# The last pair of experts as unsplit float32, through four 32-column groups of TensorE

## Chip, cores, metric

One Trainium2 chip, one of its eight cores. The metric is the device time of one execution in microseconds, median over runs. Before the change it is 2039.08 us (three runs, 2037.84 to 2042.18).

## What is computed

Two layers over 256 latent tokens and 256 context tokens of 1024 channels. Each layer mixes tokens (attention, chunked gating, Fourier), then applies a feed-forward part: dense in layer 0, a mixture of experts in layer 1. Only the mixture is touched here; it is the last thing in the program. Cut from the reference:

```python
def _swiglu(x, wg, wu, wd):
    return (jax.nn.silu(x @ wg) * (x @ wu)) @ wd

def _moe_swiglu(x, router, wg, wu, wd):
    logits = (x @ router).astype(jnp.float32)
    top_v, top_i = lax.top_k(logits, TOP_K)          # 2 of 8 experts
    top_w = jax.nn.softmax(top_v, axis=-1)
    ...
    for e in range(N_EXPERTS):
        out = out + gates[..., e:e + 1] * _swiglu(x, wg[e], wu[e], wd[e])
```

An expert has 3 x 1024 x 3584 float32 weights, 44 MB. With the given inputs the reference's router sends 200, 100, 95, 68, 42, 6, 1 and 0 tokens to the eight experts, in order of size.

## The kernel before

**Items and pairs.** Tokens are gathered by expert into items of at most 128, biggest experts first, and items are taken in pairs `a` to `d`. Here `a` is both items of the 200-token expert, `b` the 100 and 95, `c` the 68 and 42, `d` the 6 and the 1. `route` computes a number `kind` on the chip that picks one of three schedules; the first holds where pair `a` is of one expert and items 5, 6 and 7 have 64 tokens at most.

**Weights.** They come in half units of 512 KiB (128 partitions x 1024 float32): 56 per expert for gate and up (two k-tiles of 512 columns each), 28 for down (one k-tile of 1024 columns). For pairs `b`, `c`, `d` both items' half units of a step go into one 1 MiB buffer `rp`, by two transfers issued on SP's queue (line 1334); for pair `a` two successive half units of its one expert share a buffer (line 1326). There are five such buffers, so SP waits, in order, until the buffer used five steps earlier is free.

**Split.** TensorE multiplies in float32r. To keep float32 accuracy each half unit is split into hi (ScalarE, line 1311) and lo = raw - hi (VectorE, line 1312), five buffers of each; the lo of a half unit is the last reader of its raw. The generator `expert_halves` yields these parts in the order of the schedule, two ahead of their use.

**Products.** A full item takes three products per k-tile, hi*hi, hi*lo and lo*hi (`mm3`, lines 241 to 243; for pair `a`, which runs transposed with the weights stationary, line 1355). An item of at most 64 tokens puts the hi and lo parts of its tokens side by side as one 128-column stationary operand, which leaves two products (lines 1405, 1406) and a later addition of the two 64-row halves (lines 1399, 1400). Pair `c` has one full and one such item ('mixed'); pair `d` has two ('small', `gate_up_small`).

**Order.** A schedule is a string: `du01+au3` means gate/up chunks 0 and 1 of pair `d` interleaved evenly with chunk 3 of pair `a`; `d` as second letter is the down projection, `p` the gathering of a pair's tokens. Inside each schedule's block a scheduler then orders the instructions of each engine. `weighed` scales the down projection's result by the tokens' gate weights into hi and lo, `scatter` multiplies it by one-hot rows back to token places (line 1260), `residual_half` adds it to x (lines 809, 810), and `g_final` follows the last pair with the norm (lines 1284, 1287) and the output.

Of the kernel before, what the change touches and what calls it, by code (L numbers as in the profile page):

```python
# [9 lines left out]
F32 = mybir.dt.float32  # L10
# [18 lines left out]
    'bu0123456 cp ap bd0123456 cu01+au0 cu23+au1 cu4 cu56+ad01 dp cd0123456+au2 du01+au3 ad2 du2+au4 '  # L29
    'du3+au5 du4+au6 du56+ad3456 dd0123456',  # L30
# [10 lines left out]
class Act:  # L41
    """A [256 tokens, 128*n channels] activation, channel-major, as hi and lo parts, 4 k-tiles to a tile."""
# [10 lines left out]
class Joint:  # L53
    """Channel-major hidden activations of both streams, blocks 0, 1 of L, then of C, 2 k-tiles to a tile."""
# [10 lines left out]
class Pair:  # L65
    """Two items. kind:
    'whole': the hidden activations are kept until all of them are there, and then go through the down projection,
    'one': both are of one expert, and the hidden activations go through the down projection in parts,
    'small': both have 64 tokens at most, whose hi and lo parts are the two halves of the stationary operand, so that
    the hi and lo parts of the weights take two passes, and the sums of both halves are taken afterwards,  # L70
    'mixed': the first as in 'whole', the second as in 'small'."""

    def __init__(self, kind):
        self.kind, self.flat, self.aT, self.sums, self.work, self.done = kind, {}, {}, None, {}, 0
        self.shared = None
        self.small = {'small': (True, True), 'mixed': (False, True)}.get(kind, (False, False))
# [15 lines left out]
class Side:  # L92
    """Work that is emitted a step at a time between the weight units of the main stream."""
# [45 lines left out]
class Net:  # L139
# [135 lines left out]
    def linear(self, act, units, n, outs, k0=0, first=True, last=True):  # L275
        """out[b] += act[:, k0 * 128:]^T @ units; outs: (block, psum)"""
# [19 lines left out]
    def stats_by_sum(self, x, sums):  # L296
        """minus the mean [128, 1] and 1 / std [128, 1] over the 1024 channels of x; sums: of the channels, one or two"""
# [11 lines left out]
    def stats(self, x, st=None):  # L309
        """mean [128, 1] and 1 / std [128, 1] over the 1024 channels of x; st: the statistics of its halves"""  # L310
# [16 lines left out]
    def row(self, src, r=None):  # L327
        """a [1024] DRAM row on all partitions"""
# [27 lines left out]
    def mod_bias(self):  # L356
        """the biases of the modulation by channel, one added where they are of a scale"""
# [96 lines left out]
    def mod_col(self, l, s, which, kt):  # L454
        """(scale + 1, shift) of channel tile kt: which=0 before the mixer, 1 before the FFN"""
# [14 lines left out]
    def x_turned(self, xn, kt2):  # L470
        """PSUM [128, 2, 256]: channel tiles 2 kt2 and 2 kt2 + 1 of the normalised tokens"""
# [15 lines left out]
    def g_modulate(self, act, tiles, l, s, which, t4=None, kind=None):  # L487
        """act gets the modulated tiles that tiles(kt2) gives, [128, 2, 256] each"""
        for kt2 in range(4):
            if kt2 % 2 == 0:  # L490
                if kind == 'small':
                    act.h.append(self.t4([128, 4, 256], F32R))
                else:
                    self.act_tiles(act, t4)
# [3 lines left out]
            if kind == 'small':  # L498
                self.split_halves(act.h[-1][:, o, :], t)
            elif kind == 'mixed':  # L500
# [15 lines left out]
    def modulate(self, works, l, s, which, queue=None):  # L516
        """norm and modulation of stream s once the works are done, as side work"""
# [13 lines left out]
    def headnorm(self, z, nh, out, w, blk):  # L531
        """out [128, nh, 64] = rms-normed heads of z, gained, rotated when blk is a latent block"""
# [84 lines left out]
    def g_attention(self, s, sq, skv):  # L617
# [103 lines left out]
    def g_transposed(self, act, src, n, scale=1.0, c0=0):  # L721
        """append channel tiles c0..c0+n of a token-major activation to act: src(block, channel tile) is [128, 128]"""
# [58 lines left out]
    def out_kept(self, aT, ps, w, b, u):  # L781
        """block b times unit u of an output projection whose halves w are on chip"""
# [5 lines left out]
    def merge(self, l, y, n, hh, ts, acc, first, mid=None):  # L788
        """acc += 2 sigmoid(z) * (y @ w_branch), ts = tanh(z / 2); mid: what to emit after the products"""
# [31 lines left out]
    def finish(self, s, psums, rows, alpha=ALPHA, queue=None):  # L821
        """the residual now, the norm as side work"""
# [13 lines left out]
    def mixer(self, l, s, act, kv_c=None, early=None):  # L836
        """kv_c: keys and values of the context; early: what to emit while the first half of act is worked on"""
# [73 lines left out]
    def ffn(self, sL, sC):  # L911
        """the dense SwiGLU of both streams, on each weight unit together where that is possible: the first columns
        are worked on for L alone, when C may not be there yet, and the last rows of the down projection for L and
        then for C, so that L can go on. Returns what does the last rows of a stream."""
# [3 lines left out]
        def up(c, ss):  # L918
            """512 columns, the last time 256, as channels by tokens"""
# [89 lines left out]
    def moe_consts(self):  # L1009
# [7 lines left out]
        it = ld('iota', [128, 4, 128])  # L1017
# [927 lines left out]
```

## Time and profile before

| | us |
|---|---|
| median of three runs | 2039.08 |
| span of the profiled execution, first to last instruction | 2036.6 |
| TensorE busy in it | 1965.7 |
| VectorE busy | 1537.9 |
| ScalarE busy | 1258.9 |

The profiled execution's own time is its span, 2036.6 us; what lies around the span is not in the profile, and the median of the timed runs is 2.5 us above it. Busy TensorE time is that of overlapping records, so a share near 100% says that there is always a matmul in the array, not that the array is at its peak. The mixture of experts takes the part from about 1110 us to the end; the transfers of all its weights are 308 MB.

### The profile page before, as it was taken

Reading aid. Unit: us, or ns where it says so; the run is one execution under the profiler, and the core shown is the slowest. Engines: PE = TensorE matmul, PEld = TensorE weight load, DVE = VectorE, ACT = ScalarE, POOL = GpSimd, SP = SyncE. Lnnn points to the kernel's source line nnn. Section 1 sums busy time; section 2 is a strip of 40 time slices with the busy share of each in tenths; the row PEclk is TensorE's granted clock in tenths of the full one; section 3 lists DMA queues with packets and bytes.
Section 4 is the critical chain, followed back from the end, with each engine's and each line's share of the span. In section 5 each row is a group of like instructions: output and inputs, shape, how many; then the busy total and the mean of one; then the engine's idle time right before and its main releaser. Section 6 shows DMA issues by size and latency. Waiting matters only on the chain. (4 is left out here: it accounts for less than half of the span.)

```text
span 2036.6 us, 30525 instructions
## 1 busy us (share of the span) xinstructions
PE 1965.7 (97%) x10833; PEld 1627.3 (80%) x10833; DVE 1537.9 (76%) x2148; ACT 1258.9 (62%) x1653; POOL 56.6 (3%) x54
## 2 busy tenths in 40 slices
PE   6999999999999999999996999999999999999995
PEld 3788877788979979878885777888877888898863
DVE  3877776778243343798787888899898889999897
ACT  4667545655222222466763877887777878777775
POOL 0100010000000000111000000000000000000000
PEclk9999999999999999999997999999999999999998
DMA  9653566677443343444441999898899898999995
GB/s 337 242 192 138 191 243 231 220 272 261 187 175 145 145 145 128 175 158 166 145 167 61 402 358 349 325 370 318 333 349 351 324 382 325 340 326 340 336 352 203
DMA packets 119353, 519.91 MB, mean 255 GB/s; under 512 B 14688, under 2 KB 15584, under 8 KB 96144
## 3 DMA queue, kind: packets, MB, share of 16 engines
q1 hardware_dynamic: 119184, 517.80, 69.2%
q8 instruction: 89, 1.46, 0.3%
q14 instruction: 80, 0.66, 0.1%
HBM read 516.63 MB, written 1.11 MB: 254 GB/s over the span
## 5 line engine op out<-in xcount | busy, mean ns | idle before, releaser
L1312 DVE TENSOR_TENSOR lo<-rp,hi 128x1024 fp32r<-128x1024 f32 x588 | 688.3, 1219 | 66.2 <-ACT hi L1311 61.4
L1311 ACT ACTIVATE hi<-rp 128x1024 fp32r<-128x1024 f32 (+1 forms) x588 | 595.2, 1055 | 123.4 <-PE mm L1355 46.1
L242 PE MATMUL mm<-lo,t 128*128 128x512 f32 (+1 forms) x1560 | 608.4, 390 | 3.0 <-DVE lo L1312 2.0
L243 PE MATMUL mm<-hi,t 128*128 128x512 f32 (+1 forms) x1560 | 605.7, 389 | 0.7 <-DVE t L236 0.7
L241 PE MATMUL mm<-hi,t 128*128 128x512 f32 (+1 forms) x1560 | 587.8, 395 | 7.6 <-ACT hi L235 3.6
L236 DVE TENSOR_TENSOR lo<-raw,hi 128x1024 fp32r<-128x1024 f32 x268 | 325.8, 1219 | 266.3 <-ACT hi L235 265.5
L235 ACT ACTIVATE hi<-raw 128x1024 fp32r<-128x1024 f32 x268 | 282.6, 1058 | 373.6 <-PE mm L243 192.1
L241 PEld LDWEIGHTS mm<-hi,t 128*128 128x128 f32 x1560 | 292.3, 188 | 88.1 <-issue 17.5
L242 PEld LDWEIGHTS mm<-lo,t 128*128 128x128 f32 x1560 | 293.6, 188 | 67.4 <-DVE lo L1312 8.2
L243 PEld LDWEIGHTS mm<-hi,t 128*128 128x128 f32 x1560 | 293.6, 188 | 61.7 <-DVE t L236 1.3
L942 PE MATMUL mm<-t,hi 128*128 128x256 f32 x1408 | 236.6, 285 | 0.0
L942 PEld LDWEIGHTS mm<-t,hi 128*128 128x128 f32 x1408 | 200.9, 191 | 14.4 <-issue 8.4
L1406 PE MATMUL mm<-lo,t 128*128 128x512 f32 x504 | 191.7, 407 | 5.7 <-DVE lo L1312 5.7
L1405 PE MATMUL mm<-hi,t 128*128 128x512 f32 x504 | 188.5, 399 | 0.7 <-ACT hi L1311 0.7
L1355 PE MATMUL mm<-t,hi 128*128 128x256 f32 x896 | 158.4, 280 | 0.1
L942 PE MATMUL mm<-t,lo 128*128 128x256 f32 x704 | 157.4, 283 | 0.0
L1355 PEld LDWEIGHTS mm<-t,hi 128*128 128x128 f32 x896 | 137.2, 188 | 7.0 <-ACT hi L1311 0.5
L1406 PEld LDWEIGHTS mm<-lo,t 128*128 128x128 f32 x504 | 91.8, 189 | 39.4 <-DVE lo L1312 23.4
L1355 PE MATMUL mm<-t,lo 128*128 128x256 f32 x448 | 118.2, 280 | 0.0
L942 PEld LDWEIGHTS mm<-t,lo 128*128 128x128 f32 x704 | 116.5, 191 | 0.0
L1405 PEld LDWEIGHTS mm<-hi,t 128*128 128x128 f32 x504 | 94.9, 189 | 21.5 <-ACT hi L1311 2.0
L293 POOL TENSOR_TENSOR sm<-sm,mhalf 128x1 f32<-128x1 f32 (+3 forms) x46 | 54.4, 1182 | 1644.0 <-DVE sm L301 927.7
(267 smaller groups left out, 1641.2 us busy)
## 6 DMA issues: line engine op xcount, KB each, us to landing
rp<-in_expu SPq DMA_DIRECT2D x588, 512.0 KB
raw<-in_w_inu SPq DMA_DIRECT2D x64, 1024.0 KB
raw<-in_w_modu SPq DMA_DIRECT2D x44, 1024.0 KB
raw<-in_ffnu SPq DMA_DIRECT2D x42, 1024.0 KB
raw<-in_w_branchu SPq DMA_DIRECT2D x18, 1024.0 KB
raw<-in_w_outu SPq DMA_DIRECT2D x12, 1024.0 KB
t<-gd SPq DMA_DIRECT2D x9, 512.0 KB
t<-in_w_modu SPq DMA_DIRECT2D x8, 512.0 KB
```

The lines of the kernel that those rows point to most:

```text
L235: self.nc.scalar.activation(hi, src, AF.Copy)
L236: self.nc.vector.tensor_sub(lo, src, hi.bitcast(F32))
L241: mm(out, ah, wh, start=first, stop=False)
L242: mm(out, ah, wl, start=False, stop=False)
L243: mm(out, al, wh, start=False, stop=last)
L293: self.nc.gpsimd.tensor_tensor(r, ve, self.mhalf[:, :n], op=OP.pow)
L942: nc.tensor.matmul(out(t, i), a, x[i][p], start=kt + m + i + t % per == 0, stop=kt + m + i + t % per == 10)
L1311: nc.scalar.activation(hf, rs, AF.Copy)
L1312: nc.vector.tensor_sub(lf, rs if rv is None else rv, hf.bitcast(F32))
L1355: nc.tensor.matmul(out, a, x[p], start=kt + q + t % 2 == 0, stop=kt + q + t % 2 == 10)
L1405: self.nc.tensor.matmul(out, x[0], w[0], start=first, stop=False)
L1406: self.nc.tensor.matmul(out, x[0], w[1], start=False, stop=last)
```

## The change

Pair `d` becomes a kind of its own, 'tiny', for two items of 32 tokens at most. Its weights are not split: TensorE reads the raw float32 buffers. The tokens stay float32 as well. Item 0 uses output rows 0 to 63 and item 1 rows 64 to 127; each item's weight half unit is cut in two column halves, so that four matmuls with 32 stationary columns each stand in four column groups of the array. `route` tests items 6 and 7 against 32 tokens in addition. The schedule's stages from `du` on are rearranged. Gathering, gate weights, `weighed` and `scatter` get a branch for the new kind. The core of the diff:

```diff
-    'bu0123456 cp ap bd0123456 cu01+au0 cu23+au1 cu4 cu56+ad01 dp cd0123456+au2 du01+au3 ad2 du2+au4 '
-    'du3+au5 du4+au6 du56+ad3456 dd0123456',
+    'bu0123456 cp ap bd0123456 cu01+au0 cu23+au1 cu4 cu56+ad01 dp cd0123456+au2 du0123+au34 du456+ad234 '
+    'dd0123+au56 dd45+ad56 dd6',
...
-        few, k = self.sm([128, 8]), self.sm([128, 2])
-        V.scalar_tensor_tensor(few, p[:, 16:24], 64.5, a[:, 2 * STATIC_PAIRS - 3, :], op0=OP.is_gt, op1=OP.mult)
-        V.tensor_reduce(k[:, 0:1], few, op=OP.add, axis=AX.X)
+        few, k = self.sm([128, 2, 8]), self.sm([128, 2])
+        for i, most in ((0, 64.5), (1, 32.5)):
+            V.scalar_tensor_tensor(few[:, i, :], p[:, 16:24], most, a[:, 2 * STATIC_PAIRS - 3 + i, :],
+                                   op0=OP.is_gt, op1=OP.mult)
+        V.tensor_reduce(k[:, 0:1], few.rearrange("p a b -> p (a b)"), op=OP.add, axis=AX.X)
...
     def scatter(self, ys, GT, alpha, b, hh, sums=None):
         p = self.mmps()
-        for i in range(2):
+        if 'tiny' in ys:
             for k in range(2):
-                self.nc.tensor.matmul(p, GT[:, i, b * 128:(b + 1) * 128], ys[i, hh][k],
-                                      start=i + k == 0, stop=i + k == 2)
+                self.nc.tensor.matmul(p, GT[:, hh, b * 128:(b + 1) * 128], ys['tiny'][k], start=k == 0, stop=k == 1)
...
             for i in range(2):
                 nc.sync.dma_start(raw[:, i, :], self.I['expu'][ds(ex[i], 1), u].squeeze(0),
-                                  **({'cond': ldb['sync']} if i else {}))
+                                  **({'cond': ldb['sync']} if i and j not in tiny else {}))
+            if j in tiny:
+                yield from ((i, raw[:, i, :], None) for i in range(2))
+                continue
             yield 0, *parts(u, raw[:, 0, :])
...
-    def gate_up_small(self, P, c):
...
+    def gate_up_tiny(self, P, c):
+        nc = self.nc
+        if c % 4 == 0:
+            P.shared = self.t4([128, 4, 2, 128])
+        for w in range(2):
+            z = self.mmps((128, 256))
             for k in range(0, 8, 2):
                 yield
+                raws = [r.rearrange("p (m n) -> p m n", m=2) for _, r, _ in islice(self.stream, 2)]
+                for m in range(2):
+                    for i in range(2):
+                        x = P.act[:, k + m, 64 * i:64 * i + 32]
+                        for h in range(2):
+                            o = 64 * i + 32 * h
+                            nc.tensor.matmul(z[o:o + 32, :], x, raws[i][:, m, h * 256:(h + 1) * 256],
+                                             start=k + m == 0, stop=k + m == 7)
+                self.tick()
+                self.tick()
...
+    def down_tiny(self, P, cs):
+        if P.py is None:
+            P.py = self.mmps()
+        for c in cs:
+            for k in range(4):
...
+                raws = [r for _, r, _ in islice(self.stream, 2)]
+                for i in range(2):
+                    x = t[:, q, 64 * i + 32 * h:64 * i + 32 * h + 32]
+                    for hh in range(2):
+                        o = 64 * i + 32 * hh
+                        self.nc.tensor.matmul(P.py[o:o + 32, :], x, raws[i][:, hh * 512:(hh + 1) * 512],
+                                              start=c + k == 0, stop=c + k == 9)
...
+        if P.kind == 'tiny':
+            y = self.t4([128, 2, 512], F32R)
+            nc.scalar.activation(y[:, 0, :], py, AF.Copy, scale=gate[:, 0:1])
+            nc.vector.scalar_tensor_tensor(y[:, 1, :], py, gate[:, 0:1], y[:, 0, :].bitcast(F32),
+                                           op0=OP.mult, op1=OP.subtract)
+            return {'tiny': (y[:, 0, :], y[:, 1, :])}, GT
```

How the instructions move is shown at three places.

TensorE, before, where a half unit of `a` (line 1355, weights stationary) and one of `d` (lines 1405 and 1406, `hi` and `lo` the split weights, `t_15297` and `t_15343` the tokens) stand beside each other in the gate/up stages:

```order
L1355 MATMUL mm<-t_12403,lo 128x256
L1406 MATMUL mm<-lo,t_15297 128x512
L1405 MATMUL mm<-hi,t_15297 128x512
L1406 MATMUL mm<-lo,t_15297 128x512
L1405 MATMUL mm<-hi,t_15297 128x512
L1355 MATMUL mm<-t_12403,hi 128x256
```

After, in the same stages (line 1383 is line 1355 of before, line 1509 the matmul of `gate_up_tiny`, `rp` the raw weights):

```order
L1383 MATMUL mm<-t_12404,hi 128x256
L1509 MATMUL mm<-rp,t_15298 32x256 x6
L1383 MATMUL mm<-t_12405,hi 128x256
L1383 MATMUL mm<-t_12404,lo 128x256 x2
L1383 MATMUL mm<-t_12404,hi 128x256
L1383 MATMUL mm<-t_12405,hi 128x256
L1509 MATMUL mm<-rp,t_15298 32x256 x2
L1383 MATMUL mm<-t_12404,lo 128x256
```

Two products of 512 columns per k-tile and item have become four matmuls of 256 columns with 32 stationary columns for both items. They stand in bursts between the work on `a`: 91 bursts in all, down projection included, from 1 to 30 matmuls long, and 42 of them are of two, which use two of the four column groups.

SP's queue, before, in the stages of `d`: every first transfer into a buffer waits for VectorE, the reader of the raw weights that comes last (the DMAHW semaphores are those of earlier transfers):

```order
L1334 DMA rp<-in_expu 128x1024 [waits DMAHW5_49,DVE_49]
L1334 ISA
L1334 DMA rp<-in_expu 128x1024 [waits DMAHW6_49]
L1334 ISA
L1334 DMA rp<-in_expu 128x1024 [waits DMAHW7_49,DMAHW0_49,DVE_49]
```

After, a little behind the first transfers of `d` (line 1351 is a buffer of `a`, line 1359 one of a pair):

```order
L1359 DMA rp<-in_expu 128x1024 [waits DMAHW3_49,PE_49]
L1359 ISA
L1359 DMA rp<-in_expu 128x1024 [waits DMAHW4_49]
L1351 ISA
L1351 DMA rp<-in_expu 128x1024 [waits DMAHW5_49,DVE_49]
L1351 ISA
L1351 DMA rp<-in_expu 128x1024 [waits DMAHW6_49]
L1359 ISA
L1359 DMA rp<-in_expu 128x1024 [waits DMAHW7_49,PE_49]
```

A transfer that follows a buffer of `d` now waits for TensorE, whose matmuls read it; one that follows a buffer of `a` still waits for VectorE.

TensorE at the very end, after (line 1544 is the matmul of `down_tiny`, line 1284 the scatter of the other pairs, here `a`, line 1280 that of `d`):

```order
L1544 MATMUL mm<-rp,t_17182 32x512 x2
L1284 MATMUL mm<-t_18520,GT 128x512 x2
L1284 MATMUL mm<-t_18523,GT 128x512
L1284 MATMUL mm<-t_18526,GT 128x512
L1284 MATMUL mm<-t_18523,GT 128x512
L1284 MATMUL mm<-t_18526,GT 128x512
L1544 MATMUL mm<-rp,t_17182 32x512 x2
L1284 MATMUL mm<-t_18526,GT 128x512 x2
L1544 MATMUL mm<-rp,t_17182 32x512 x6
L1280 MATMUL mm<-t_18590,GT 128x512 x8
```

The scatter of `a` now lies between the last four steps of `d`; before it lay among the 28 steps of `dd0123456`. The scatter of `d` is 8 matmuls, before 16.

## Rows read from the trace of the kernel before

**Rows 1.** Busy time by stretch: engines, granted clock, DMA share, GB/s.

```profile
core 0: us, PE busy (x) PEld busy (x) DVE busy (x) ACT busy (x) POOL busy (x), PEclk, DMA share, GB/s
1100.00:1110.00 10.00, 1.99 (x14) 1.83 (x13) 6.96 (x42) 0.00 (x0) 0.00 (x0) 0.50 0.00 1
1120.00:1160.00 40.00, 39.02 (x173) 30.55 (x174) 35.17 (x39) 33.76 (x41) 0.00 (x0) 1.00 1.03 409
1160.00:1270.00 110.00, 109.15 (x486) 86.61 (x485) 93.38 (x89) 83.81 (x98) 0.00 (x0) 1.00 0.97 359
1742.00:1850.00 108.00, 108.00 (x723) 98.66 (x722) 99.29 (x101) 81.77 (x94) 0.00 (x0) 1.00 0.92 330
1925.00:1985.00 60.00, 55.16 (x213) 39.55 (x212) 57.78 (x60) 46.48 (x49) 0.00 (x0) 0.94 0.95 351
1985.00:2003.00 18.00, 17.60 (x63) 10.24 (x63) 18.00 (x17) 14.97 (x15) 0.00 (x0) 1.00 1.02 405
...
1664.00:2003.00 339.00, 331.65 (x1789) 274.81 (x1788) 314.24 (x316) 262.26 (x291) 0.00 (x0) 0.99 0.93 342
```

**Rows 2.** Waits from 1100 us to the end: total us, times, longest.

```profile
SPq L1334 <- DVE lo L1312: 424.8, 224, 6.5
...
ACT hi L1311 <- PE mm L1355: 46.1, 36, 2.2
...
ACT hi L1311 <- DMA rp<-in_expu: 7.8, 24, 2.7
```

**Rows 3.** TensorE in order of time, in a stage of d and a.

```profile
1752.39 0.39 PE L1405 MATMUL mm<-hi,t 128*128 128x512 f32 x1
1752.62 0.40 PE L1406 MATMUL mm<-lo,t 128*128 128x512 f32 x1
...
1754.13 0.40 PE L1355 MATMUL mm<-t,hi 128*128 128x256 f32 x2
...
1754.48 0.40 PE L1355 MATMUL mm<-t,hi 128*128 128x256 f32 x2
```

**Rows 4.** Groups by line from 1675 to 2011 us: count, busy, mean ns.

```profile
L1312 DVE TENSOR_TENSOR lo<-rp,hi 128x1024 fp32r<-128x1024 f32 x222 | 259.5, 1219 | 20.2 <-ACT hi L1311 19.3
...
L1406 PE MATMUL mm<-lo,t 128*128 128x512 f32 x338 | 129.8, 412 | 5.2 <-DVE lo L1312 5.2
L1405 PE MATMUL mm<-hi,t 128*128 128x512 f32 x339 | 127.2, 400 | 0.7 <-ACT hi L1311 0.7
L1355 PE MATMUL mm<-t,hi 128*128 128x256 f32 x512 | 90.9, 280 | 0.1
...
L242 PE MATMUL mm<-lo,t 128*128 128x512 f32 x84 | 33.2, 395 | 0.0
...
L1260 PE MATMUL mm<-t,GT 128*128 128x512 f32 x32 | 8.7, 399 | 1.3 <-DVE t L1597 1.3
```

**Rows 5.** Transfers of lines 1334 and 1326 from 1664 us on.

```profile
L1334 SPq DMA_DIRECT2D rp<-in_expu x168: 332/333/1677, 1664.4 to 2000.8; - x168
...
L1326 SPq DMA_DIRECT2D rp<-in_expu x52: 332/333/1386, 1668.4 to 1915.7; - x52
```

**Rows 6.** TensorE in order of time around a burst of line 425.

```profile
32.65 0.39 PE L243 MATMUL mm<-hi,t 128*128 128x512 f32 x1
32.97 1.92 PE L425 MATMUL sd<-t,cT 128*32 128x512 f32 x16
34.83 0.50 PE L241 MATMUL mm<-hi,t 128*128 128x512 f32 x1
...
35.41 0.40 PE L243 MATMUL mm<-hi,t 128*128 128x512 f32 x1
```

**Rows 7.** The chain of work that ended last, its last pieces.

```profile
2010.93 0.70 ACT t L1596
2011.67 0.73 PE mm L1260 x2
...
2013.40 2.07 DVE t L1597 x3
2015.47 1.19 DVE t L809 x2
```

More of the change, by code (lines that the diff above doesn't have):

```diff
@@ L1216, in gathered @@
                     for i in range(2):
-                        nc.tensor.matmul(p[:, m, :], self.xs[b][i][:, c], G[b], start=b + i == 0, stop=b + i == 2)
-            return p
+                        nc.tensor.matmul(p[:, m, :], self.xs[b][i][:, c], G[b][:, :n], start=b + i == 0,
+                                         stop=b + i == 2)
+            return p
+        if kind == 'tiny':
+            act = self.t4([128, 8, 128])
+            for kt2 in range(4):
+                self.modulated(act[:, 2 * kt2:2 * kt2 + 2, :], gathered(kt2), 1, 'L', 1, kt2)
+                yield
+            return act, G
         act = Act()
@@ L1246, in g_pair_gates @@
         p = self.trps([128, 2, 2])
+        gate = self.gp.tile([128, 2], F32, name="gslot", tag="gslot")
+        if tiny:
+            for i in range(2):
+                for h in range(2):
+                    for b in range(2):
+                        nc.tensor.matmul(p[:, i, :], G[b][:, h * 128:(h + 1) * 128], gs[:, i, b, :],
+                                         start=h + b == 0, stop=h + b == 2)
+            for i in range(2):
+                s = slice(64 * i, 64 * i + 64)
+                V.tensor_reduce(gate[s, 0:1], p[s, i, :], op=OP.add, axis=AX.X)
+            yield
+            return GT, gate
         for i in range(2):
@@ L1257, in scatter @@
         p = self.mmps()
-        for i in range(2):
+        if 'tiny' in ys:
             for k in range(2):
-                self.nc.tensor.matmul(p, GT[:, i, b * 128:(b + 1) * 128], ys[i, hh][k],
-                                      start=i + k == 0, stop=i + k == 2)
+                self.nc.tensor.matmul(p, GT[:, hh, b * 128:(b + 1) * 128], ys['tiny'][k], start=k == 0, stop=k == 1)
+        else:
+            for i in range(2):
+                for k in range(2):
+                    self.nc.tensor.matmul(p, GT[:, i, b * 128:(b + 1) * 128], ys[i, hh][k],
+                                          start=i + k == 0, stop=i + k == 2)
         self.residual_half(self.x['L'][b], hh, p, self.m5, alpha, sums)
@@ L1499, in gate_up_small @@
             for k in range(0, 8, 2):
                 yield
-                for i, hi, lo in islice(self.stream, 2):
-                    for m in range(2):
-                        kt = k + m
-                        self.mm_item(P, i, z[i], P.act.parts(kt, i), (hi[:, m, :], lo[:, m, :]), kt == 0, kt == 7)
-                    self.tick()
-            if w == up:
-                self.need(P.flat[c])
-            P.flat[c] = self.spawn_first(w(z))
+                raws = [r.rearrange("p (m n) -> p m n", m=2) for _, r, _ in islice(self.stream, 2)]
@@ new lines, in gate_up_tiny @@
+                for m in range(2):
+                    for i in range(2):
+                        x = P.act[:, k + m, 64 * i:64 * i + 32]
+                        for h in range(2):
+                            o = 64 * i + 32 * h
[3 more added lines that the diff above has]
+                self.tick()
+            if w == 0:
+                g = self.u2([128, 256])
+                nc.scalar.activation(g, z, AF.Silu)
+            else:
+                nc.vector.tensor_mul(g, g, z)
@@ new lines, in turned @@
+        def turned(out):
+            p = self.trps([128, 2, 128])
+            for q in range(2):
+                self.tr(p[:, q, :], g[:, q * 128:(q + 1) * 128])
+            nc.scalar.activation(out, p, AF.Copy)
+            yield
+        P.aT[c] = P.shared
+        P.flat[c] = self.spawn_first(turned(P.shared[:, c % 4]))
+    def down_tiny(self, P, cs):
[3 more added lines that the diff above has]
+            for k in range(4):
+                yield
+                if k == 0:
+                    self.need(P.flat.pop(c))
+                    t = P.aT.pop(c)[:, c % 4]
+                h, q = divmod(k, 2)
+                raws = [r for _, r, _ in islice(self.stream, 2)]
+                for i in range(2):
+                    x = t[:, q, 64 * i + 32 * h:64 * i + 32 * h + 32]
[3 more added lines that the diff above has]
+                                              start=c + k == 0, stop=c + k == 9)
+                self.tick()
+                self.tick()
+        return P.py
@@ L1662, in experts @@
         if small:
-            kinds.update({STATIC_PAIRS - 2: 'mixed', STATIC_PAIRS - 1: 'small'})
-        work = {'whole': self.gate_up, 'one': self.gate_up_one, 'small': self.gate_up_small,
-                'mixed': self.gate_up_mixed}
+            kinds.update({STATIC_PAIRS - 2: 'mixed', STATIC_PAIRS - 1: 'tiny'})
+        work = {'whole': self.gate_up, 'one': self.gate_up_one, 'mixed': self.gate_up_mixed, 'tiny': self.gate_up_tiny}
         def prep(j):
@@ L1708, in experts @@
         steps = [t for t in order if t[0][1] != 'p']
-        self.stream = ahead(self.expert_halves([(t[i][0], u) for t in steps for i, u in merged(t)], one),
-                            2)
+        self.stream = ahead(self.expert_halves([(t[i][0], u) for t in steps for i, u in merged(t)], one,
+                                               [j for j in kinds if kinds[j] == 'tiny']), 2)
         pairs, sc, alpha = {}, None, ALPHA
@@ L1722, in experts @@
                     pairs[j] = self.start_pair(preps.pop(j), gms[:, j], kinds.get(j, 'whole'))
-                g = self.down(pairs[j], cs, last) if w == 'd' else up(pairs[j], w, cs)
+                tiny = pairs[j].kind == 'tiny'
+                g = up(pairs[j], w, cs) if w != 'd' else \
+                    self.down_tiny(pairs[j], cs) if tiny else self.down(pairs[j], cs, last)
                 next(g)
@@ L1921, in host_arrays @@
     t = np.arange(256, dtype=f).reshape(2, 2, 64)
-    out['iota'] = np.tile(np.stack([t[:, :1].repeat(2, 1), t], 1).reshape(1, 4, 128), (128, 1, 1))
+    it = np.stack([t[0], t[1, :1].repeat(2, 0), t[1]]).reshape(3, 128)
+    tiny = np.full((2, 2, 2, 32), -1e6, f)
+    for h in range(2):
+        tiny[h, :, h] = t[:, 0, :32]
+    out['iota'] = np.tile(np.concatenate([it, tiny.reshape(2, 128)])[None], (128, 1, 1))
     out['iota_e'] = np.tile(np.arange(8, dtype=f), (128, 2, 1))
```

55 lines of the change are left out of this document (13 added, 42 removed).

## The prediction

> **What bounds the kernel now.** I read the busy time by stretch first, then the waits, then single engines in order of time. From 1664 us, where the first weights of pair `d` are asked for, to 2003 us TensorE is busy 331.65 of 339 us and the weights come in at 342 GB/s [rows 1]. That alone doesn't say which of the two sets the pace, since the DMA share is high as well. The waits do: ScalarE waits for a raw buffer to land only 24 times, 7.8 us in all, but for a buffer that TensorE still reads much longer, and SP's queue stands 424.8 us until VectorE has freed a raw buffer [rows 2]. So the transfers are held back by the consumers. In the stages where `d` and `a` alternate the consumer is TensorE: 108.00 us busy of 108, VectorE at 99.29 [rows 1]. What the queue can do when buffers are free is seen twice: 409 GB/s over 40 us at the start of the experts, and 405 GB/s in the 18 us from 1985 us [rows 1].
>
> How much work TensorE has there: matmuls of 512 columns start every 0.23 us, those of 256 columns every 0.117 us (three in 0.35 us) [rows 3]. By the code `d` has 84 half-unit pairs x 8 = 672 of the former, which make up nearly all of the 677 that lines 1405 and 1406 show from 1675 us on; `a` has 768 of the latter (the 512 shown are two thirds of them) and, with five chunks of down projection left, 240 of the former; 32 are of scatter [rows 4]. That is 155 + 90 + 55 + 7 = 307 us. The last 28 steps are not TensorE's: two subtractions of 1.219 us per step [rows 4], 2.44 us, exceed 8 x 0.23 = 1.84 us, which adds 17 us. The sum of 324 us explains the stretch of 339.
>
> **The change, part by part.**
>
> *The matmuls of d.* Removed: 672 x 0.23 = 155 us. Added: 448 of 32 x 256 and 112 of 32 x 512, in float32. The trace of before has this very form: line 425 sends 16 matmuls of 128*32, 512 columns, through the four column groups, and TensorE, from the start of line 243 at 32.65 to that of another at 35.41, spends 2.76 us on them and on three ordinary matmuls [rows 6]. Three of 0.23 us leave 2.07 us. The first of the 16 starts at 32.97 and the next ordinary matmul at 34.83, 1.86 us, so a group of four takes at most 0.46 us; I take 0.43, which leaves 0.35 us for entering and leaving the four-group form. Were the four one after another, 16 would take 16 x 0.43 = 6.9 us, which excludes that here. So whole groups cost 112 x 0.215 + 28 x 0.43 = 36 us. The order has 91 bursts, 42 of them of two matmuls, which leave half of the groups empty: about 18 x 0.215 + 14 x 0.43 = 10 us more for the groups that are cut, and 91 x 0.35 = 32 us of entering and leaving. In all 78 us; bounds are 36 us and, one after another, 448 x 0.215 + 112 x 0.43 + 32 = 176 us. TensorE's work in the section falls from 307 to 152 + 78 = 230 us.
>
> *The splits of d.* 168 subtractions and as many copies to hi go: 205 us of VectorE at 1.219 us. They matter for themselves only in the last stage (17 us above); elsewhere TensorE covered them. The additions of the two halves go too, under the same cover.
>
> *What is late next: the transfers.* Their number doesn't change: 168 + 52 transfers of 512 KiB from 1664.4 us on [rows 5], 115.3 MB. With TensorE at 230 us this becomes the bound: 282 us at 409 GB/s, 337 us at the 342 of the whole stretch. I take 400 GB/s, 288 us: in the new order up to four of five buffers can be on their way while TensorE reads the fifth, as at the start of the experts, where the 409 was seen; the small discount is for stretches such as `dd0123+au56`, where a step of `d` and one of `a` bring 1.5 MiB (3.9 us) and hold TensorE for 24 x 0.117 + about 0.8 = 3.6 us.
>
> *The wait that is added.* A transfer into a buffer that `d` used waits for TensorE's matmuls instead of VectorE. Behind it on SP stand all later transfers, of `a` too. TensorE runs its program in order, so when it works on two half units of `a` in a row, 2 x 2.8 us, four buffers (10.5 us of transfers) still cover it. At the beginning they don't: the first buffers of `d` are full before TensorE has finished `c`. For that I put 4 us.
>
> *The end.* After the last weights have landed, before, two more steps were split and multiplied; the residual additions began at 2015.47 us, and 21.1 us later the span ended [rows 7]. Now: one group 0.43, ScalarE 0.70, VectorE about 0.7 (2.07 us for three), TensorE 0.73, 2.6 us from landing to the same point. But the last half units of `a` are multiplied only some 5 MiB, 13 us, before the last landing, and VectorE then has the rest of `a` in front of it: two splits, four additions, four passes of `weighed`, eight residual passes of about 0.6 us each, with TensorE between, some 19 us. That is 6 us after the last landing. I take 6.5, so 27.6 us from last landing to the end of the span.
>
> *Small parts.* One more VectorE operation in `route`, 64 KB more of constants, half as many columns in gathering `d`: each below 2 us, of both signs, hidden by TensorE's work on `c` or too small; nothing.
>
> *The sum.* 1664.4 + 4 + 288 + 1 for the last landing + 27.6 = 1985.0 us, against a span of 2036.6: 51.6 us less. Everything before 1664.4 us stays. The median of the runs is 2039.08, 2.5 above this span; 2039.1 - 51.6 gives 1987.5, say **1987 us**.
>
> **The rivals.**
>
> *The transfers don't go that fast (0.18).* For it: the long stretch from 1160 us ran at 359 GB/s with a DMA share of 0.97, that from 1925 us at 351 with 0.95 [rows 1], so the DMA engines look full there. Against it: SP waited for free buffers in those stretches, and the 409 and 405 stand at shares of 1.03 and 1.02. At 355 GB/s the section takes 325 us: 1664.4 + 4 + 325 + 1 + 27.6 = 2022, 14.6 less than before, 2024. At 375, 2007.
> The Trainium skill, "DMA: Bandwidth & Descriptors", section "Where 436 GB/s comes from", says that for transfers from HBM the HBM share of a core, about 358 GB/s, binds. By that page the weights would take 322 us and the time would be about 2021 us, in this rival. The 409 GB/s over 40 us in this case's rows, with one core running, is above it.
>
> *The groups don't overlap when they are cut into bursts between other matmuls (0.09).* Line 425 stands in bursts of 16; here most are shorter. With 176 us TensorE keeps 328 us in this section, as much as the 324 now; the end may save 3 us. That gives 2035 to 2041, no change.
>
> *Slower: TensorE loses its clock (0.05).* It will have 230 us of work in some 290, where it had 307 in 339. The granted clock was 0.50 in the 10 us from 1100 us, when it had 1.99 us of work, and 0.94 from 1925 us, when it was held back by others [rows 1]. At the lower of the two levels, 1.2 GHz, its 230 us become 460, past the transfers: 136 us longer than the 324 of now, about 2175. It decides from a mean granted clock of 230 / 324 = 0.71 down. Against it: once TensorE is late, it has no gaps left, and at 17.60 busy of 18 us the clock was 1.00 [rows 1]; and where it waits for transfers, a slow half unit of `a` (5.6 us) with two of `d` still fits into the 6.6 us that their 2.5 MiB take.
> The Trainium skill, "TensorE: Matmul & The Clock Gate", section "Why this matters for your kernels", warns of pauses in the stream of matmuls that put the array back to half clock. The row at 0.50 agrees; whether pauses as short as here do it, no row of before shows.
>
> *The change doesn't do what it says (0.02).* If items 6 and 7 had over 32 tokens, `route` would pick the second schedule, where `c` and `d` are whole pairs: 84 x (2 + 4) more matmuls of 0.23 us, +116 us. The router's counts for these inputs end in 6, 1, 0.
>
> **How the numbers follow.** Forecast 0.66, the rivals 0.18, 0.09, 0.05, 0.02. The likeliest case by itself spans from 1971 (409 GB/s, no loss at the beginning, 24 us at the end: 1664.4 + 282 + 1 + 24 = 1971.4 of span, 1974 of time, less 3 for the small parts) to about 2003 (380 GB/s, 303 us). To leave out no more than 2 in 10 the range takes in most of the first rival: **1971 to 2024**. A measurement of this kernel tells a change of about 0.2% (4 us) from none. Faster: the forecast, the first rival and 0.04 of the second, 0.88; same 0.04; slower 0.08.
>
> **What would show it.** After 1664 us: GB/s near 400 instead of 342, TensorE clearly idle, its idle time ended by transfers of `rp`; SP waiting for TensorE less than it waited for VectorE; bursts of lines 1509 and 1544 at 0.22 or 0.43 us per four; the last transfer issued near 1955 us; VectorE finishing `a` at the end while the last weights are already there. It is wrong if GB/s stays near 360, if the granted clock falls below 0.9 in these stretches, or if TensorE is still busy throughout.

## The result, and the profile after

The changed kernel takes **2011.95 us** (median of 4 runs, 2011.09 to 2014.26) against 2039.24 for the kernel before on the same chip: ratio 0.9864, 95% interval 0.9852 to 0.9876. That is 27 us less, where 52 were forecast. The profiled execution's span is 2010.9 us, and the section of `d` and `a` begins at 1664.8 us, as before; all of the difference lies behind that point.

Busy time by stretch of the changed kernel, cut at its stages; columns as in [rows 1], which it answers:

```profile
core 0: us, PE busy (x) PEld busy (x) DVE busy (x) ACT busy (x) POOL busy (x), PEclk, DMA share, GB/s
1664.00:1700.00 36.00, 34.81 (x245) 26.11 (x244) 24.15 (x30) 15.66 (x19) 0.00 (x0) 1.00 0.89 328
1700.00:1773.00 73.00, 67.13 (x663) 45.90 (x662) 15.74 (x17) 15.91 (x23) 0.00 (x0) 1.00 1.01 395
1773.00:1850.00 77.00, 66.66 (x558) 39.66 (x558) 18.28 (x19) 15.44 (x20) 0.00 (x0) 1.00 1.03 409
1850.00:1925.00 75.00, 70.61 (x480) 46.23 (x477) 24.42 (x25) 20.64 (x24) 0.00 (x0) 0.98 0.98 366
1925.00:1962.00 37.00, 36.68 (x207) 22.32 (x207) 12.34 (x13) 8.53 (x10) 0.00 (x0) 1.00 0.87 309
1962.00:1979.00 17.00, 17.00 (x79) 8.89 (x79) 6.55 (x9) 4.79 (x6) 0.00 (x0) 1.00 0.98 375
1979.00:1987.00 8.00, 8.00 (x38) 3.08 (x34) 5.14 (x9) 0.00 (x0) 0.00 (x0) 1.00 0.21 84
```

From 1700 to 1850 us it goes as forecast: 395 and 409 GB/s, with TensorE idle in between. From 1850 us, in the stages `dd0123+au56` and `dd45+ad56`, TensorE is the busy one again and the rate falls to 366 and 309. The weights have landed by 1979 us (84 GB/s over the next 8 us are 0.67 MB, less than the two reads of line 332, 1 MiB, that are issued behind the last weights), and TensorE works on for 8 us.

The waits of SP's queue from 1664 us on (us, times, longest), which answer [rows 2], and the longest of the kernel before in the same section:

```profile
SPq L1359 <- PE mm L1509: 68.0, 32, 5.0
SPq L1351 <- PE mm L1544: 36.1, 10, 4.8
...
SPq L1351 <- DVE lo L1337: 22.9, 15, 3.5
SPq L1359 <- PE mm L1544: 15.6, 8, 5.2
SPq L1359 <- DVE lo L1337: 13.9, 8, 4.2
```
```profile
SPq L1334 <- DVE lo L1312: 174.6, 79, 5.1
```

It is now mostly TensorE that holds the raw buffers, 119.7 us with its matmuls of `d` (lines 1509 and 1544); VectorE still does for 36.8 us. The groups of instructions of 1675 to 2011 us, in place of [rows 4]:

```profile
L1509 PE MATMUL mm<-rp,t 128*32 128x256 f32 x896 | 68.4, 384 | 1.9 <-DMA rp<-in_expu 1.8
L1337 DVE TENSOR_TENSOR lo<-rp,hi 128x1024 fp32r<-128x1024 f32 x54 | 65.0, 1223 | 124.9 <-ACT hi L1336 124.4
...
L1544 PE MATMUL mm<-rp,t 128*32 128x512 f32 x224 | 44.4, 603 | 0.0
```

The subtractions fell from 222 to 54, as they should. But lines 1509 and 1544 stand with 896 and 224 records, and by the code they issue 448 and 112 matmuls: **each float32 matmul leaves two records**. TensorE in order of time, around a burst of four matmuls of line 1544 (eight records) and one of two (four records):

```profile
1883.40 1.07 PE L1544 MATMUL mm<-rp,t 128*32 128x512 f32 x8
1884.40 0.74 PE L1383 MATMUL mm<-t,hi 128*128 128x256 f32 x4
...
1896.59 0.40 PE L1383 MATMUL mm<-t,hi 128*128 128x256 f32 x2
1896.91 1.05 PE L1544 MATMUL mm<-rp,t 128*32 128x512 f32 x4
1897.89 0.50 PE L1383 MATMUL mm<-t,hi 128*128 128x256 f32 x2
1898.23 0.28 PE L1383 MATMUL mm<-t,lo 128*128 128x256 f32 x1
```

From its start to that of the next ordinary matmul the full group of four takes 1.00 us, and the half group of two takes 0.98: a half-empty group costs as much as a full one. Transfers and the last chain, in place of [rows 5] and [rows 7]:

```profile
L1359 SPq DMA_DIRECT2D rp<-in_expu x168: 332/333/1407, 1664.8 to 1971.9; - x168
```
```profile
1985.58 1.86 PE mm L1544 x12
...
1988.21 1.45 PE mm L1280 x5
1989.68 2.48 DVE t L806 x4
```

The last weights are asked for at 1971.9 us (forecast: near 1955). The residual additions begin at 1989.68 us, 21.2 us ahead of the end, as before.

### The profile page after: what moved, and what is told of

Its sections match the earlier page's. It is cut to its first block, busy times and chain, and to the rows that moved or that the text cites. A ratio compares the mean times of both kernels' runs of the same rounds, so it can differ in the third digit from the quotient of the medians.

```text
span 2010.9 us, 30473 instructions
## 1 busy us (share of the span) xinstructions
PE 1924.3 (96%) x11263; PEld 1538.0 (76%) x11263; DVE 1319.2 (66%) x1940; ACT 1067.3 (53%) x1450; POOL 56.6 (3%) x54
## 5 line engine op out<-in xcount | busy, mean ns | idle before, releaser
L1337 DVE TENSOR_TENSOR lo<-rp,hi 128x1024 fp32r<-128x1024 f32 x420 | 494.1, 1221 | 172.2 <-ACT hi L1336 168.0
L1336 ACT ACTIVATE hi<-rp 128x1024 fp32r<-128x1024 f32 (+1 forms) x420 | 425.5, 1056 | 88.8 <-PE mm L245 39.6
L243 PEld LDWEIGHTS mm<-hi,t 128*128 128x128 f32 x1560 | 291.7, 188 | 101.7 <-issue 20.0
L244 PEld LDWEIGHTS mm<-lo,t 128*128 128x128 f32 x1560 | 294.2, 189 | 76.5 <-DVE lo L1337 12.4
L245 PEld LDWEIGHTS mm<-hi,t 128*128 128x128 f32 x1560 | 294.2, 189 | 62.5 <-issue 1.6
L939 PE MATMUL mm<-t,hi 128*128 128x256 f32 x1408 | 236.6, 284 | 0.0
L1383 PE MATMUL mm<-t,hi 128*128 128x256 f32 x896 | 166.3, 285 | 4.9 <-ACT hi L1336 4.9
L939 PEld LDWEIGHTS mm<-t,lo 128*128 128x128 f32 x704 | 116.6, 192 | 0.0
L1383 PEld LDWEIGHTS mm<-t,lo 128*128 128x128 f32 x448 | 81.1, 188 | 11.6 <-DVE lo L1337 7.7
L248 PE MATMUL tr<-ident,t 128*128 128x128 f32 x376 | 60.0, 283 | 18.6 <-ACT t L326 16.8
L248 PEld LDWEIGHTS tr<-ident,t 128*128 128x128 f32 x376 | 45.6, 144 | 37.7 <-ACT t L326 21.2
L1509 PE MATMUL mm<-rp,t 128*32 128x256 f32 x896 | 68.4, 384 | 1.9 <-DMA rp<-in_expu 1.8
```

What stands on the lines that cost most here:

```text
L243: mm(out, ah, wh, start=first, stop=False)
L244: mm(out, ah, wl, start=False, stop=False)
L245: mm(out, al, wh, start=False, stop=last)
L248: self.nc.tensor.transpose(out, src, self.ident)
L939: nc.tensor.matmul(out(t, i), a, x[i][p], start=kt + m + i + t % per == 0, stop=kt + m + i + t % per == 10)
L1336: nc.scalar.activation(hf, rs, AF.Copy)
```

## The experiments

My theory after the result: a four-group of 512 columns costs 0.86 us, not 0.43, so TensorE is the bound where a step of `d` stands beside each step of `a`. Rivals: the wait for raw buffers, a price per burst or group that doesn't depend on columns, the order of the stages, the clock. Every time below is a median; before ran at 2039.9 to 2040.3 beside them. In the table a stage lasts from the issue of its first weight transfer on SP to that of the next stage (the transfers of lines 1351 and 1359 counted in the program's order); "forecast" is its number of transfers at 400 GB/s, with 4 us in the first.

| stage (transfers) | forecast | changed | whole groups | half columns | six buffers | one pass |
|---|---|---|---|---|---|---|
| du0123+au34 (80) | 108.9 | 108.6 | 106.1 | 108.8 | 109.1 | 105.2 |
| du456+ad234 (60) | 78.6 | 77.2 | 78.6 | 77.1 | 76.0 | 78.3 |
| dd0123+au56 (48) | 62.9 | 74.8 | 65.9 | 70.4 | 71.1 | 69.6 |
| dd45+ad56 (24) | 31.5 | 36.9 | 31.7 | 34.2 | 38.6 | 31.9 |

**Whole groups.** The second item's matmuls are issued first and the first item's behind them, so that no burst begins with half of the groups: 57 bursts in place of 91, none of two matmuls.

```diff
+                r = mms(1)
+                with self.tc.issue_after(r.ins):
+                    mms(0)
```

> The new kernel, in which the matmuls on the second item's weights come first in a step and those on the first item's must follow them, so that no burst holds half of the column groups (57 bursts instead of 91, none of two). Same arithmetic. Theory P: in the two stages dd0123+au56 and dd45+ad56 a step loses a half-empty group of 0.86 us and an entry and exit of about 0.3 us; they become as fast as the transfers allow (about 3.9 to 4.1 us per step instead of 4.65), 14 to 18 us less, and the last four steps 3 us: 1990 to 1998 us. Theory B: no gain, or a loss, since the first matmul waits longer for its weights: 2010 to 2018 us.

The kernel takes **1993.35 us**, ratio 0.9771 (0.9755 to 0.9788), which is in the theory's range. The two stages fall to 65.9 and 31.7 us. By stretch, and TensorE around a burst of eight matmuls (16 records):

```profile
1849.00:1915.00 66.00, 62.11 (x479) 45.52 (x480) 24.89 (x25) 19.80 (x23) 0.00 (x0) 0.97 1.03 408
1915.00:1947.00 32.00, 32.00 (x207) 22.02 (x206) 12.31 (x13) 9.52 (x10) 0.00 (x0) 1.00 0.97 366
```
```profile
1935.34 1.92 PE L1548 MATMUL mm<-rp,t 128*32 128x512 f32 x16
1937.20 1.20 PE L243 MATMUL mm<-hi,t 128*128 128x512 f32 x4
```

Eight matmuls, two whole groups, take 1.86 us, to the hundredth what the "16 matmuls" of [rows 6] took; those were eight too. Against 1.00 for one group, a further group takes 0.86. That leaves 0.12 us of the 0.98 above; the two ordinary matmuls before that burst and the two behind it took 0.32 and 0.34 us in place of 0.23, so that entering and leaving cost about 0.3 us in all, as an estimate from these rows. The edit takes away half-empty groups and entries together and doesn't separate the two: in the time of the two stages TensorE has 20 bursts in place of 32, and 12 x 0.3 are 3.6 of the 14.1 us by which the stages fell.

**Half columns.** `d`'s down projection multiplies 256 of each 512 columns; the other half of its output is left out (zeros).

```diff
-    matmul(P.py[o:o + 32, :], x, raws[i][:, hh * 512:(hh + 1) * 512],
+    matmul(P.py[o:o + 32, 0:256], x, raws[i][:, hh * 512:hh * 512 + 256],
```

> The new kernel, but the down projection of d multiplies only the first 256 of each 512 columns: half of the output columns of d are left out, so the output isn't the reference's. Transfers, bursts and waits stay. Theory P: about 28 x 3.4 x 0.215 = 20 us of TensorE go, nearly all in stages that it bounds: 1991 to 1998 us. Theory B: no change, 2008 to 2014 us.

The kernel takes **1999.6 us**, ratio 0.98 (0.9784 to 0.9817), 1.6 above the theory's range and 8 below the rival's. A burst of four matmuls, here of 256 columns:

```profile
1890.67 0.64 PE L1545 MATMUL mm<-rp,t 128*32 128x256 f32 x8
1891.24 0.73 PE L1383 MATMUL mm<-t,hi 128*128 128x256 f32 x4
```

It takes 0.57 us in place of 1.00, so half of the columns cost 0.43 less: the price goes by columns. The kernel gains 12 us, where I had put about 20 us of TensorE's time.

**One pass.** The same matmuls on the upper 16 bits of each operand.

```diff
+    x = P.act[:, k + m, 64 * i:64 * i + 32].bitcast(BF16)[:, 1::2]
...
+    raws[i][:, m, h * 256:(h + 1) * 256].bitcast(BF16)[:, 1::2],
```

> The changed kernel, in which the four-group matmuls of d read only the upper 16 bits of each float32 weight and activation (as bfloat16, every other 2-byte element): the lower 16 bits of both are left out of d's products. Number, columns and order of the matmuls stay. P, my theory (a float32 matmul of a four-group is two passes of 0.43 us for 512 columns): each of them then leaves one record, not two, 560 in place of 1120; a four-group of 512 columns takes about 0.22 us, entering and leaving a burst still costs 0.3; a step of d beside one of a takes TensorE some 3.7 us, below the transfers' 3.85; the stages dd0123+au56 and dd45+ad56 go from 74.8 and 36.9 to 62 to 67 and 31 to 33 us; 1988 to 1998 us in all. Rival B: the price is one of the groups or bursts, not of float32; then the stages stay above 70 and 35 us and the time at 2005 to 2014.

The kernel takes **1992.22 us**, ratio 0.9765 (0.9749 to 0.9781). Groups of 1664 to 2011 us, then TensorE around bursts of two, four and six matmuls, and the stretch from 1850 us:

```profile
L1510 PE MATMUL mm<-rp,t 128*32 128x256 bf16 x448 | 29.1, 282 | 7.1 <-DMA rp<-in_expu 6.9
L1545 PE MATMUL mm<-rp,t 128*32 128x512 bf16 x112 | 16.3, 403 | 0.0
```
```profile
1939.10 0.40 PE L1545 MATMUL mm<-rp,t 128*32 128x512 bf16 x2
1939.43 0.51 PE L246 MATMUL mm<-hi,t 128*128 128x512 f32 x1
1939.87 0.41 PE L1545 MATMUL mm<-rp,t 128*32 128x512 bf16 x4
1940.21 0.97 PE L244 MATMUL mm<-hi,t 128*128 128x512 f32 x3
...
1946.55 0.63 PE L1545 MATMUL mm<-rp,t 128*32 128x512 bf16 x6
1947.11 1.20 PE L244 MATMUL mm<-hi,t 128*128 128x512 f32 x4
```
```profile
1850.00:1918.00 68.00, 59.19 (x403) 48.30 (x402) 22.85 (x24) 18.30 (x22) 0.00 (x0) 0.90 1.00 388
```

One record for each matmul, 448 and 112. Two of 512 columns take 0.33 us to the next start and four 0.34, so the groups do work side by side. Six, which are two groups, take 0.56: a further group is 0.22 us, a quarter of the 0.86 in float32, and it is float32 that makes the price. The time is in the theory's range; the stage `dd0123+au56`, at 69.6 us, isn't. There the granted clock was 0.90 on average (1850 to 1918 us). The scheduler also placed these bursts otherwise (97), so this run doesn't say which of the two held that stage.

**Six raw buffers**, four of the low parts.

```diff
-    self.weight_pools(5, 5, 0):
+    self.weight_pools(6, 5, 0):
```

> The new kernel with six raw buffers of 1 MiB instead of five, and four lo buffers instead of five to make room. Theory P: the transfers run further ahead at the beginning of the section, worth at most 4 us, and the stages that TensorE bounds stay as they are; the missing lo buffer may cost as much: 2006 to 2016 us. Theory B: GB/s in the stages dd0123+au56 and dd45+ad56 rises from 300 to 350 towards 400: 1992 to 2002 us.

The kernel takes **2009.24 us**, ratio 0.9846 (0.983 to 0.9863), in the theory's range. A sixth buffer alone doesn't bring the two stages to the transfers' rate: they take 71.1 and 38.6 us, 109.7 together against 111.7. The low-part buffer that is missing may hide a small part of a gain; this run doesn't show how much.

**Order and format apart.** First the changed kernel with the stages of before, then before with stages near the new ones:

```diff
-    du0123+au34 du456+ad234 dd0123+au56 dd45+ad56 dd6
+    du01+au3 ad2 du2+au4 du3+au5 du4+au6 du56+ad3456 dd0123456
```

> The new kernel with the stages of pair d in the order of before (du01+au3 ad2 du2+au4 du3+au5 du4+au6 du56+ad3456 dd0123456). Theory P (TensorE's price: a group of four float32 matmuls of 512 columns takes 0.86 us, two records of 0.43, so that TensorE and not the transfers sets the pace wherever a step of d meets a step of a): the stages with one step of a per step of d stay bound by TensorE, about 34 us per 8 steps, the last 28 steps of d alone run at the pace of the transfers, 2.56 us each; the section is about as long as in the new kernel (308 us), but nothing of a is left at the end, so the tail after the last transfer shrinks from 39 to about 28 us: 2000 to 2008 us. Theory B (too few raw buffers: the transfers are held back because five buffers are not given back in time, whatever TensorE's work is): no change beyond the tail's few us, 2005 to 2012 us. That the order of stages is itself the gain: 2030 us or more.

The kernel takes **2024.26 us**, ratio 0.992 (0.9904 to 0.9937), which is above the ranges of P and B and below the third. By stretch, `du3+au5`, `du4+au6`, and `dd0123456` by itself; then `du3+au5` in the kernel before:

```profile
1771.00:1808.00 37.00, 35.29 (x320) 26.75 (x319) 12.12 (x13) 11.48 (x15) 0.00 (x0) 1.00 0.94 349
1808.00:1846.00 38.00, 36.29 (x328) 27.77 (x327) 12.68 (x15) 11.04 (x14) 0.00 (x0) 1.00 0.93 336
...
1917.00:1989.00 72.00, 63.76 (x294) 18.14 (x292) 12.89 (x19) 5.18 (x7) 0.00 (x0) 1.00 1.00 392
```
```profile
1772.50:1810.30 37.80, 37.80 (x263) 34.90 (x262) 34.38 (x35) 29.39 (x35) 0.00 (x0) 1.00 0.95 326
```

Eight steps of `d` beside eight of `a` take 37 to 38 us here too, 4.6 to 4.75 a step (I had put 34 us): the old order has more of these. The kernel before, with `d` split, needed 37.8 us for the same eight steps: beside `a`, unsplit weights in cut groups give almost nothing. Counted from issue to issue, 4.6 us of the gain lie in each of the stages `du56+ad3456` and `dd0123456`. Where `d` is alone, the transfers set the pace, and the clock stays at 1.00 while TensorE waits for them.

```diff
-    du01+au3 ad2 du2+au4 du3+au5 du4+au6 du56+ad3456 dd0123456
+    du0123+au34 du456+ad234 dd0123+au56 ad56 dd456
```

> The kernel of before, with d's weights still split into bfloat16 parts, and its stages brought near the new order: du0123+au34, du456+ad234, dd0123+au56, ad56, dd456 (dd45 beside ad56 is not possible there, since a split d needs more of PSUM). P, my theory: the new order by itself spreads VectorE's splits, so its 17 us of waits mostly go, but the 307 us of TensorE in [rows 1] stay and bound the section; ad56 stands alone again. About 2022 to 2036 us, that is 4 to 17 us below before. Rival: the order is the whole gain of the change and the float32 of d gives nothing; then about 2012 us.

The kernel takes **2044.82 us**, ratio 1.0025 (1.0015 to 1.0035), slightly slower than before; both sides missed. (The parts of `d` are float32r, `fp32r` in the rows, not bfloat16.) From 1734 to 1838 us:

```profile
1734.00:1838.00 104.00, 99.24 (x520) 79.64 (x519) 101.29 (x102) 84.14 (x98) 0.00 (x0) 1.00 0.95 361
```

With two steps of split `d` to one of `a`, VectorE's subtractions fill nearly the whole stretch, 101.29 of 104 us. So the two halves of the change aren't additive: unsplit weights alone give 16 us, an order near the new one alone costs 5, and the change gives 27.

**More even orders.** Once on the changed kernel, once with whole groups, once more with six buffers.

```diff
-    du0123+au34 du456+ad234 dd0123+au56 dd45+ad56 dd6
+    du0123+au345 du45+ad234 du6+au6 dd01234+ad56 dd56
```

> The changed kernel with its stages in an evener order: du0123+au345, du45+ad234, du6+au6, dd01234+ad56, dd56; 82 bursts of four-groups in place of 91, 34 of them of two matmuls in place of 42. P, my theory (a four-group of 512 columns takes 0.86 us, so a stage with as many steps of a as of d is bound by TensorE at 4.67 us a step, and one with more d by the transfers at 3.85): the sections come to about 126 + 63 + 37 + 62 + 20 = 308 us against 316 in the changed kernel, and less stays behind the last landing; 1997 to 2006 us. Rival: the order was no limit once d is unsplit, the time stays at 2009 to 2014.

The kernel takes **2009.31 us**, ratio 0.9849 (0.9832 to 0.9865), which is the rival's range. The first stage took 133.8 us where I had 126. The five stages together took 307.3 us from first issue to last, as I had put; but counted in the same way the changed kernel's take 307.1, not the 316 with which I compared.

> The even order (du0123+au345, du45+ad234, du6+au6, dd01234+ad56, dd56) and the whole bursts (the second item's matmuls go first and the first item's follow them), both on top of the changed kernel: 50 bursts, none of two matmuls. P: TensorE's work then falls below the transfers in every stage, the section goes at the transfers' rate of about 405 GB/s throughout, 283 to 290 us from the first issue to the last landing, plus a tail of 24.5 to 27 us: 1978 to 1986 us. Rival: whole bursts had already taken all that the order could give, the time stays at 1990 to 1996.

The kernel takes **1995.62 us**, ratio 0.978 (0.9764 to 0.9796): the rival's range again, no better than whole groups alone. Its stretches:

```profile
1668.00:1700.00 32.00, 31.87 (x224) 25.21 (x226) 23.24 (x29) 15.27 (x18) 0.00 (x0) 1.00 0.89 325
1700.00:1793.00 93.00, 86.56 (x882) 68.30 (x877) 27.95 (x29) 27.20 (x36) 0.00 (x0) 0.98 1.00 386
1793.00:1962.00 169.00, 148.93 (x1120) 94.96 (x1108) 55.84 (x62) 38.77 (x47) 0.00 (x0) 0.96 1.02 402
```

The early stage, into which I had moved 8 more steps of `a`, begins with TensorE busy throughout (31.87 of 32 us) and the transfers held back at 325 GB/s. I take it that this stage now has too little slack to catch up; no run here shows that by itself.

> The even order and the whole bursts, with six raw buffers and four of the low parts. P: where the transfers bound the section already, a further buffer has nothing to fill: within 4 us of the kernel with five raw buffers. Rival: gaps of single waits for a raw buffer are still in it, then 5 us or more below that kernel.

The kernel takes **1992.14 us**, ratio 0.9762 (0.9746 to 0.9778), 3.5 below, within what I had put.

**`a` spread behind the start.** Whole groups, with the first stage as in the changed kernel; then the same with six buffers.

```diff
-    du0123+au34 du456+ad234 dd0123+au56 dd45+ad56 dd6
+    du0123+au34 du45+ad234 du6+au5 dd012+au6 dd345+ad56 dd6
```

> Whole bursts as in the kernel with whole groups, and a's units spread another way: du0123+au34, du45+ad234, du6+au5, dd012+au6, dd345+ad56, dd6, with 8 to 12 us of slack of TensorE against the transfers in each stage but du6+au5. P: the first stage, with half as many steps of a as of d, goes at 106 us as it did there, the others at the transfers' rate (about 57, 32, 41, 41, 9); a is done earlier, so the end falls from 27.7 us after the last landing to 25 to 26; 1985 to 1992 us. Rival: the start and the end cost the same in any order; 1991 to 1996.

The kernel takes **1990.87 us**, ratio 0.9761 (0.9745 to 0.9777), in the theory's range, with the stages as put (106.1, 59.3, 31.3, 41.2 and 41.9 us) and an end of 25.8 us. But it is only 2.5 us from whole groups alone and just under the rival's range, so its gain over them is unclear.

> The kernel with whole bursts and a's units spread (du0123+au34, du45+ad234, du6+au5, dd012+au6, dd345+ad56, dd6), with six raw buffers and four of the low parts. P: as the even order gained 3.5 us by the sixth buffer, 0 to 4 us below the same with five, 1983 to 1991 us. Rival: no gain, or a loss through the missing buffer of the low parts.

The kernel takes **1983.95 us** (1982.59 to 1985.29), ratio 0.9727 (0.971 to 0.9743), the fastest of all, 28 us below the changed kernel. From 1700 to 1940 us the transfers run at their rate:

```profile
1664.00:1700.00 36.00, 34.69 (x253) 27.01 (x252) 24.49 (x30) 15.66 (x19) 0.00 (x0) 1.00 0.92 332
1700.00:1768.00 68.00, 60.89 (x647) 44.75 (x649) 15.91 (x17) 15.40 (x22) 0.00 (x0) 0.97 1.03 408
...
1857.00:1898.00 41.00, 40.43 (x346) 30.64 (x346) 14.43 (x15) 11.66 (x14) 0.00 (x0) 1.00 1.03 408
1898.00:1940.00 42.00, 37.26 (x229) 22.51 (x233) 12.29 (x12) 9.51 (x10) 0.00 (x0) 1.00 1.03 409
```
```profile
1948.83 10.15 DMA rp<-in_expu
...
1959.03 1.11 PE mm L1548 x8
```

The chain now passes through a transfer, which lands at 1958.98; the span ends 24.5 us later (1983.5). The gain of 6.9 us over the kernel with five buffers is more than the 0 to 4 I had put.

## Why the prediction was right, and its size was not

The direction held, and so did the mechanism in the stages up to 1850 us: TensorE is relieved, and the transfers set the pace. In `dd0123+au56` and `dd45+ad56` it didn't: there TensorE stayed the bound. One term was mis-sized, and most of the miss follows from it. That the range held is partly luck: the likeliest case by itself ended at about 2003, and the range reached to 2024 only for the rival of slower transfers, which did not come.

**The matmuls of d** (the term that failed). I read the 16 records of [rows 6] as 16 matmuls, that is four groups at 0.43 us. They are eight matmuls, two groups at 0.86. With that price my own sum gives 72 us for whole groups in place of 36, 20 in place of 10 for the cut ones, and about 27 for entering and leaving (91 x 0.3): 119 where I had 78. TensorE's work becomes 152 + 119 = 271 us, not 230. That is still below the transfers' 282 us (at 409 GB/s) over the whole section, but not stage by stage: a step of `d` with one of `a`, which I had at 3.6 us against 3.9 of transfers, takes 74.8 / 16 = 4.67 us. By the corrected price, as an estimate, it is 2.81 for `a` + 0.86 + 0.3 = 3.97 us where the group is whole, and 2.81 + 2 x (0.86 + 0.3) = 5.13 where it is cut in two; the measured 4.67 lies between. Without the 2.81 it leaves 1.86 us for `d`, waits included, where the split products took 8 x 0.23 = 1.84: in these stages the change relieves TensorE of next to nothing. Whole groups, half the columns and one pass each bring these stages down, which shows that the price is what holds them. Counting a line's records against the matmuls that the code issues would have told it from the trace of before: line 425 has 384 records there, and by the code it issues 192 matmuls.
The Trainium skill, "FP8 and Floating Point Precision", section "TensorE Precision Notes", says that true float32 goes through the array in four passes; an estimate by it, 4 x 512 columns at 2.4 GHz, is 0.85 us for a group. The measured 0.86 agrees, though the trace shows two records, not four.

**What is late next: the transfers.** Right where TensorE leaves room: 409 GB/s over 77 us here, 408 or 409 nearly throughout from 1700 to 1940 us in the fastest kernel. This refutes the rival of slower transfers. In `dd0123+au56` and `dd45+ad56` they were not what is late: 111.7 us against 94.4 at 400 GB/s, 17 of the 26 us by which the span missed its forecast (2010.9 against 1985.0).
The Trainium skill, "DMA: Bandwidth & Descriptors", section "Where 436 GB/s comes from", has the HBM share of about 358 GB/s bind; with one core running, the rows show 409. The Trainium skill, "HBM Reference", section "Specifications (TRN2)", says that a core that streams alone gets above that share; these rows agree with that.

**The wait that is added.** 36 us at 328 GB/s instead of 400 lose 36 x (1 - 328 / 400) = 6.5 us, where I had 4; the first stage as a whole took 108.6 of the 108.9 that I had for it.

**The end.** I had 27.6 us from the last landing; it took 2010.9 - 1979 = 32, since TensorE, late by then, worked until 1987.4 us on `d` and on the scatter of `a`. This and the stages leave some 5 of the 26 us to the last stage, where the backlog still holds buffers.

**The splits of d.** Their work went (222 subtractions to 54), as forecast; that SP waits for TensorE instead, and less, was in the list of signs: 119.7 us for the matmuls of `d`, against 174.6 for VectorE at the buffers of pairs alone. Other signs failed: the last transfer was issued at 1971.9 us instead of near 1955, a full group cost 0.43 or 0.86 us instead of 0.22 or 0.43, and TensorE was not clearly idle behind 1925 us.

**The other rivals.** Groups that don't overlap: refuted; four matmuls take 1.00 us and two 0.98. TensorE's clock: 0.98 and 1.00 in the stages that were long, far from the 0.71 at which it decides.

## What to carry to other kernels

Before a duration from the trace becomes a price, count the records of that line against the instructions that the program issues: here one matmul was two records, and the error halved the price of a group. When one engine's work is cut so that a transfer becomes the bound, compare the two stage by stage, not over the section; the stages in which the old engine still leads give back the gain. Column groups pay when all of them start together: here a half-filled group cost as much as a full one, and it paid to issue first the matmuls whose weights arrive last.

## What the runs showed of the hardware that I had not expected

- A float32 matmul through a 32-column group leaves two records and takes 0.86 us for 512 columns, two or four side by side; the same in bfloat16 leaves one and takes 0.22 us, a quarter (0.56 us for two groups, 0.34 for one).
- The granted clock fell in some of these kernels, though hardly in the changed one (0.98 or 1.00 by stretch up to 1987 us). With one pass it was 0.90 on average from 1850 to 1918 us, part of the time at 1.2 GHz in place of 2.4, where TensorE was busy 59.19 of 68 us; with the old order it stayed at 1.00 where TensorE was busy 63.76 of 72. With the even order and whole groups, at the end, where TensorE waits for each transfer, the same four matmuls take 1.93 or 1.06 us:

```profile
1969.81 1.06 PE L1548 MATMUL mm<-rp,t 128*32 128x512 f32 x8 [0.87 <-DMA rp<-in_expu]
1972.32 1.93 PE L1548 MATMUL mm<-rp,t 128*32 128x512 f32 x8 [1.44 <-DMA rp<-in_expu]
```

  The granted clock there was 0.73 (1950 to 1975 us), again a mean of the two levels. Behind the last landing this costs about 1 us, and another in the five matmuls of line 1280 that follow (2.52 us in that kernel's last chain, 1.45 in that of the changed kernel).
